# A second, smaller set of staging places, filled by GpSimd's queue, in the opening of a decoder layer

## The chip, the cores and the metric

The kernel runs on one core of a Trainium2 chip. The metric is the device time of one execution in microseconds (us), here of that core. The times of a kernel are given as the median over several runs.

## The reference

One decoder layer over 2048 tokens of width 1024, in float32. Cut to what matters:

```python
mem_n = rmsnorm(mem, mem_norm_g)                       # 256 memory tokens
h = rmsnorm(x, mix_norm_g)
q, k, v, g, u = split(h @ w_in)                        # 4 x 512 and 512 columns
y_ret  = silu(g) * head_rmsnorm(retention(q, k, v))    # 4 heads, chunks of 128
y_pool = (mean over 2/4/8/16 tokens - u) @ pool_w * pool_scale
x = x + concat(y_ret, y_pool) @ w_out
k, v = split(mem_n @ xa_wkv)                           # attention into the memory
s = (rmsnorm(x) @ xa_wq) @ k.T / 16;  p = softmax(s)   # per head
x = x + (p @ v) @ xa_wo
x = x + conv_glu_ffn(rmsnorm(x))
return rmsnorm(x, final_norm_g)
```

## The kernel before

**Products.** Each float32 operand is kept as a pair, a rounded high part and the rest, and each product is three TensorE passes: high by high (L276), high by low (L277), low by high (L278). A pair is made by a *split*: ScalarE copies the high part (L264, or L267 where a factor per row comes in), VectorE subtracts it from the source to get the low part (L248, or L256 with a factor). A split of a 128x1024 tile thus needs its source in SBUF, a place for the pair, and the two engines one after the other.

**Stages.** The first 118 us or so are the *folds*, products that depend on the memory tokens and the weights alone. `folded_weights` is a generator that runs through them in 29 steps, numbered n = 0 to 28 by the loop around it:

- K0 to K7, the key products, and V0 to V7, the value products, 24 matmuls of 128x256 each: the memory against a tile of `wkv` (L347). Two neighbouring products share a PSUM bank, which is scaled and split into a pair of its own afterwards. The banks rotate: M0's first takes the bank that K0 and K1 had.
- M0 to M3, the score products, 48 matmuls of 128x256: two rows of `wqT` per head against the keys.
- O0 to O3, the output products, 24 matmuls of 128x512 for each row of `wo` against the values.
- W0 to W3, short products of `wout_p` with the pooling weights.

They run in the order K0 to K7, V0, V1, M0, V2, M1, V3, M2, V4, M3, O0, V5, O1, V6, O2, V7, W0, W1, O3, W2, W3. Then come the two halves of 1024 tokens, each with its projections, retention, mixer, attention and feed-forward part, until the end at about 2391 us.

Between the steps of the folds the first half's x is prepared: `load_x_wide` loads tile k (128x1024, 512 KB), splits it with the norm's factors, squares it in place on ScalarE (L658), and adds it to `total` on VectorE, from which the norm is made. Tile k = 0 is itself the start of `total`. The tiles are called at the steps in `x_at`. `value_weights` loads the weights of the first products behind the folds, 512 KB a call, 128 rows at a time in each half of a place; it is called at n = 24 and 25, and twice at n = 27.

**Places.** All these loads, the rows of the folds (`load_tile`, `row_pair`), the x tiles and the value weights, go into one set of nine places of 128x1024 float32, `raws`: three in the tile R, the two tiles S (S_80, S_81 below), four in the first arena of Z (Z_75 below). `take` gives the place that was freed first by the order in which the program is written; whoever takes it waits until its last reader has gone. x0 keeps its place until the norm (n = 21), the memory tokens keep two until their norm.

**Queues.** All of these loads are issued by SyncE (SP), one after the other; an issue that waits for its place holds up those behind it. GpSimd's queue has nothing until the sums of weights in DRAM (`weight_sums`, L1055 and L1058, with small copies, L1075) that belong to the stage behind the folds.

**Order.** The Tile framework orders the instructions of each engine by a simulated timeline of its own; `keep_in_program_order` holds some instructions in the order in which they are written: an x tile's load, its split, its square and its sum among them. So a change in one load can put products of TensorE into another order.

Of the kernel before, what the change touches and what calls it, by code (L numbers as in the profile page):

```python
# [16 lines left out]
P = 128  # L17
# [4 lines left out]
T = 1024  # L22
# [120 lines left out]
def trunk(ctx, tc, xT, memT, pos, w_qkgu, w_v, wkv, wqT, wo, wout_r, wout_p, poolT, w_up, w_dn, vecs, consts, outT):  # L143
    nc = tc.nc
    pe, act, dve, pool, sp = nc.tensor, nc.scalar, nc.vector, nc.gpsimd, nc.sync
# [14 lines left out]
    def new_e(at, dtype):  # L160
        return Arena(cp.tile([P, 2 * T], dtype, tag=f"E{at}", name=nm("E")), 0, 2, T)

    def new_s(dtype, at):
        return cp.tile([P, T], dtype, tag=f"S{at}", name=nm("S"))

    B = Joined(Arena(G, 16 * T, 12, T), new_e(0, F32R), new_e(1, F32R))

    def new_z(at, dtype):
        return Arena(cp.tile([P, 4 * T + (0 if at else 4 * EDGE)], dtype, tag=f"Z{at}", name=nm("Z")), 0, 4, T)

    Z = Joined(new_z(0, F32), new_z(1, F32))
    TT = Arena(cp.tile([P, TEMPS * TW], F32, tag="T", name="T"), 0, TEMPS, TW)
    R = cp.tile([P, 3 * T], F32, tag="R", name="R")
    Q = cp.tile([P, 3 * T], F32R, tag="Q", name="Q")
    S = [new_s(F32, j) for j in range(2)]
    raws = Places([(R, j * T) for j in range(3)] + [(r, 0) for r in S], T)
# [70 lines left out]
    def tt(eng, out, a, b, op):  # L247
        return eng.tensor_tensor(out=out, in0=a, in1=b, op=op)  # L248
# [12 lines left out]
    def split(src, hi, lo, g=None, kept=False):  # L261

        if g is None:
            one = act.activation(hi, src, AF.Copy)  # L264
            two = tt(dve, lo, src, hi.bitcast(F32), ALU.subtract)
        else:
            one = act.activation(hi, src, AF.Identity, scale=g)  # L267
            two = stt(lo, src, g, hi.bitcast(F32), ALU.mult, ALU.subtract)
        if kept:
            tc.keep_in_program_order(one)  # L270
        if kept == "both":
            tc.keep_in_program_order(two)
# [7 lines left out]
    def new_raw():  # L280
        r = raws.take()
        r.free()
        return r.f
# [367 lines left out]

    def load_x_wide(k, total):

        r = total if k == 0 else raws.take()
        f = r.f
        tc.keep_in_program_order(sp.dma_start(f, xT[k * P : (k + 1) * P, :T]))
        split(f, X[:, 2 * k], X[:, 2 * k + 1], mixg[:, k : k + 1], kept="both")
        tc.keep_in_program_order(act.activation(f, f, AF.Square))  # L658
        if k:
            tc.keep_in_program_order(tt(dve, total.f, total.f, f, ALU.add))  # L660
            r.free()
# [66 lines left out]
            sp.dma_start(rope_d[i], r.f[:, :SUB])  # L728
            r.free()

    def value_weights(kp, where=None):
        raw = new_raw()
        sp.dma_start(raw.rearrange("p (k n) -> p k n", k=2), w_v[2 * kp : 2 * kp + 2].rearrange("k p n -> p k n"))
        u = (B if where is None else B.arenas[where]).take(2)
        for i in range(2):
            r = raw[:, i * SUB : (i + 1) * SUB]
            split(r, u.r[:, i * T : i * T + SUB], u.r[:, i * T + SUB : (i + 1) * T])
        return u
# [1273 lines left out]
    def rows_norm(s_acc):  # L2012
        rn = smp.tile([P, 8], F32, tag="rn", name=nm("rn"), bufs=3)
        dve.tensor_copy(rn, stats([r.f[:, : r.f.shape[1] // SUB * SUB] for r in s_acc]))
        for r in s_acc:
            r.free()
        return rn
# [67 lines left out]
        after(2, step)  # L2085

    under[0], spacing[0] = weight_sums(), 2
    raws = Places([(R, j * T) for j in range(3)] + [(r, 0) for r in S] + [(Z.arenas[0].t, j * T) for j in range(4)], T)
    results = Places([(Z.arenas[1].t, j * T) for j in range(4)], T)
    wv, total, x_at = [], raws.take(), (5, 10, 12, 13, 14, 16, 17, 18)  # L2090
    for n, _ in enumerate(folded_weights()):
        if n in x_at:
            load_x_wide(x_at.index(n), total)
        if n == 21:
            total.back = None
            rn = rows_norm([total])
        if n in (24, 25):
            wv.append(value_weights(len(wv), 0))
        if n == 27:
            wv += [value_weights(kp, kp - 1) for kp in (2, 3)]  # L2100
    rb = [TT.take() for _ in range(NS)]
    normed = (rn, rb)
    behind[0] = spread_steps(rn, [r.f[:, :SUB] for r in rb])
# [1 line left out]
    for b in range(NB):  # L2105

        if b == 0:
            raws = Places([(R, j * T) for j in range(3)] + [(r, 0) for r in S], T)
# [74 lines left out]
        for n in TURNS[first:]:  # L2183
            if n == TURNS[first]:
                raw = ahead
            else:
                raw = new_raw()
# [3 lines left out]
            if n in (5, 2, 3):  # L2191
                j = (5, 2, 3).index(n)
# [39 lines left out]
        wv, acc, place = [], [], Joined(new_e(0, F32), new_e(1, F32))  # L2232

        def opening():
            for kp in range(KT // 2):
                if kp > 1:
                    B.arenas[kp - 1] = new_e(kp - 2, F32R)
                with tc.issue_after(fetched[0].ins):
                    wv.append(value_weights(kp, (0, 0, 1, 2)[kp]))
                yield  # L2240
                yield
# [96 lines left out]
    raws = Places([(raws.one[i].t, raws.one[i].base + j * SUB) for i in raws.freed for j in range(2)], SUB)  # L2338
    E = [new_e(j, F32R).t for j in range(2)]
    Z = [new_z(j, F32).t for j in range(2)]  # L2340
# [114 lines left out]
```

## Time and profile before

| what | value |
|---|---|
| runs | 2396.65, 2393.47, 2395.16 us; median 2395.16 |
| profiled execution | 2392.77 us, its span 2391.0 us |
| mean granted TensorE clock | 0.998 of full speed |
| busy share of the span | TensorE 99%, its weight load 83%, VectorE 75%, ScalarE 58%, GpSimd 14% |
| DMA | 527.78 MB, mean 221 GB/s |

The span is what the profile's rows cover; the execution's time has 1.8 us more around it. Rows of the order of time hold the start in us, the duration, the engine, the line, the operation, the output and the inputs by the program's names without their numbers, and in brackets the idle time of the engine just before, with what ended it. "PE" is TensorE, "DVE" VectorE, "ACT" ScalarE, "POOL" GpSimd, "SPq" the instructions with which SP issues transfers. R, S and Z in such a row can be any of the places above.

### The profile page before, as it was taken

The numbers are of one execution on the slowest core, as the hardware profiler recorded it, in microseconds if no ns is written. First come the engines' busy times: TensorE is split into PE (matmuls) and PEld (weight loads), VectorE is DVE, ScalarE is ACT, GpSimd is POOL, SyncE is SP. The second block draws the span as 40 slices with busy tenths as digits, with TensorE's granted clock in tenths as the row PEclk, the third lists the DMA queues.
The fourth block names the chain that finished last, engine by engine and source line by source line (L and its number), as shares of the span: only waits on it lengthen the run. The fifth ranks groups of instructions, "written<-read, shape, count | busy, mean of one in ns | idle before, by whom it ended". The sixth has DMA issues, their size and how long they took to land.

```text
span 2391.0 us, 33436 instructions
## 1 busy us (share of the span) xinstructions
PE 2370.1 (99%) x11136; PEld 1981.2 (83%) x11136; DVE 1795.9 (75%) x2977; ACT 1387.2 (58%) x2507; POOL 337.1 (14%) x524
## 2 busy tenths in 40 slices
PE   9999999999999999999999999999999999999998
PEld 8788888888888888888888888888888888888886
DVE  7777776885667677776788776977677698867876
ACT  6854554664445455536555555855555577666663
POOL 0055554454041000000001010110000000000000
PEclk9999999999999999999999999999999999999999
DMA  8999999999595234477467564765455479758952
GB/s 305 332 280 295 275 259 288 298 296 313 179 249 134 80 107 166 155 270 236 168 235 258 176 195 132 251 202 176 152 177 187 132 259 318 235 181 287 342 174 74
DMA packets 269453, 527.78 MB, mean 221 GB/s; under 512 B 30048, under 2 KB 50912, under 8 KB 269280
## 3 DMA queue, kind: packets, MB, share of 16 engines
q1 hardware_dynamic: 212176, 402.83, 50.7%
q0 software_dynamic: 40960, 94.40, 16.6%
q10 hardware_dynamic: 16144, 28.43, 3.2%
q8 instruction: 87, 1.43, 0.2%
q14 instruction: 86, 0.70, 0.1%
HBM read 423.30 MB, written 196.61 MB: 259 GB/s over the span
## 4 chain that ended last, share of the span: by engine, by line
PE 92%; DMA 4%; DVE 2%; ACT 1%; issue 1%; SPq 0%; ACTq 0%; DVEq 0%
PE mm L276 29%; PE mm L278 29%; PE mm L277 29%; PE aux L276 1%; PE aux L278 1%; PE aux L277 1%; DMA S<-w_v 1%; PE aux L804 1%; PE aux L778 1%; PE aux L789 1%; PE aux L951 1%; PE aux L806 1%; PE aux L357 0%; DMA R<-wout_r 0%; DMA R<-Md 0%
## 5 line engine op out<-in xcount | busy, mean ns | idle before, releaser
L276 PE MATMUL mm<-G,Q 128*128 128x512 f32 (+1 forms) x1445 | 559.3, 388 | 6.0 <-ACT Q L264 2.3
L277 PE MATMUL mm<-G,Q 128*128 128x512 f32 (+1 forms) x1445 | 559.3, 387 | 0.3 <-DVE G L256 0.2
L278 PE MATMUL mm<-G,Q 128*128 128x512 f32 (+1 forms) x1445 | 555.8, 387 | 0.0
L277 PE MATMUL mm<-G,E 128*128 128x512 f32 (+1 forms) x1072 | 409.3, 382 | 0.0
L276 PE MATMUL mm<-G,E 128*128 128x512 f32 (+1 forms) x1072 | 408.3, 382 | 0.9 <-ACT E L264 0.5
L278 PE MATMUL mm<-G,E 128*128 128x512 f32 (+1 forms) x1072 | 407.6, 382 | 1.0 <-DVE E L248 1.0
L276 PEld LDWEIGHTS mm<-G,Q 128*128 128x128 f32 x1445 | 272.0, 188 | 62.3 <-ACT Q L264 2.7
L277 PEld LDWEIGHTS mm<-G,Q 128*128 128x128 f32 x1445 | 272.1, 188 | 54.6 <-DVE G L256 0.7
L278 PEld LDWEIGHTS mm<-G,Q 128*128 128x128 f32 x1445 | 271.7, 188 | 54.2 <-DVE Q L248 0.2
L248 DVE TENSOR_TENSOR Z<-Z,mm 128x512 f32<-128x512 f32 (+1 forms) x290 | 193.1, 670 | 92.8 <-PE mm L278 91.2
L256 DVE SCALAR_TENSOR_TENSOR Z<-Z,vecs,Z 128x1024 f32<-128x1024 f32 x176 | 224.5, 1279 | 50.6 <-ACT Z L1223 47.2
L278 PEld LDWEIGHTS mm<-G,E 128*128 128x128 f32 x1072 | 201.3, 188 | 40.6 <-DVE E L248 1.4
L276 PEld LDWEIGHTS mm<-G,E 128*128 128x128 f32 x1072 | 201.4, 188 | 40.3 <-DVE Z L248 0.7
L277 PEld LDWEIGHTS mm<-G,E 128*128 128x128 f32 x1072 | 201.5, 188 | 39.1
L248 DVE TENSOR_TENSOR Q<-R,Q 128x512 fp32r<-128x512 f32 (+2 forms) x206 | 141.0, 685 | 88.0 <-ACT Q L1160 46.9
L248 DVE TENSOR_TENSOR T<-T 128x512 f32<-128x512 f32 (+4 forms) x196 | 133.7, 688 | 28.3 <-ACT T L424 13.6
L1160 ACT ACTIVATE Q<-R 128x512 fp32r<-128x512 f32 (+1 forms) x123 | 75.8, 617 | 131.7 <-PE mm L277 126.1
L1160 ACT ACTIVATE E<-R 128x512 fp32r<-128x512 f32 (+1 forms) x163 | 100.3, 615 | 71.5 <-PE mm L277 56.8
L1223 ACT ACTIVATE Z<-Z,vecs 128x1024 f32<-128x1024 f32 x88 | 109.1, 1241 | 33.8 <-DVE Z L248 32.8
L1107 ACT ACTIVATE G<-T 128x512 fp32r<-128x512 f32 x180 | 108.1, 623 | 34.5 <-DMA T<-Gd 24.9
L1160 ACT ACTIVATE Q<-S 128x512 fp32r<-128x512 f32 (+1 forms) x81 | 49.9, 616 | 97.6 <-PE mm L277 95.2
L248 DVE TENSOR_TENSOR Q<-S,Q 128x512 fp32r<-128x512 f32 (+1 forms) x112 | 75.8, 677 | 37.9 <-ACT Q L1160 26.5
(425 smaller groups left out, 4415.8 us busy)
## 6 DMA issues: line engine op xcount, KB each, us to landing
T<-Gd SPq DMA_DIRECT2D x168, 256.0 KB, 4.5
Ud<-w_up POOLq DMA_DIRECT2D x132, 256.0 KB, 9.9
Gd<-Z SPq DMA_DIRECT2D x110, 256.0 KB, 2.6
R<-Ud SPq DMA_DIRECT2D x104, 256.0 KB, 2.7
R<-w_up SPq DMA_DIRECT2D x82, 256.0 KB, 2.9
S<-Ud SPq DMA_DIRECT2D x72, 256.0 KB, 2.8
Gd<-T SPq DMA_DIRECT2D x56, 256.0 KB, 3.4
T<-Xd SPq DMA_DIRECT2D x53, 256.0 KB, 4.2
```

The source lines that it names most:

```text
L248: return eng.tensor_tensor(out=out, in0=a, in1=b, op=op)
L256: return dve.scalar_tensor_tensor(out=out, in0=a, scalar=s, in1=b, op0=op0, op1=op1)
L276: pe.matmul(ps, lh, rh, start=start, stop=False, skip_group_check=more)
L277: pe.matmul(ps, lh, rl, start=False, stop=False, skip_group_check=more)
L278: latest[0] = pe.matmul(ps, ll, rh, start=False, stop=stop, skip_group_check=more)
L778: pe.matmul(col(sc, c), self.ch(k, c), self.ch(q, c), start=True, stop=True)
L789: pe.matmul(col(kv, c), col(self.kn.f, c), self.ch(v, c, h * T), start=True, stop=True)
L804: pe.matmul(col(y, c), col(self.pr.f, c), self.ch(v, c, h * T), start=True, stop=self.cur[c] is None)
L806: pe.matmul(col(y, c), self.ch(q, c), self.cur[c], start=False, stop=True)
L1107: one = act.activation(hi, x, AF.Copy, scale=-1.0 if i == 2 else 1.0)
L1160: act.activation(p2[:, 0, :w], self.raw[i].f[:, :w], AF.Copy)
L1223: act.activation(self.c[g].f, a[:, 2:], AF.Identity, bias=cb[:, f : f + 1], scale=cw[2][:, f : f + 1])
```

## The change

The x tiles and the four loads of value weights get a set of places of their own, `side_raws`, two of the four in Z's arena; `raws` keeps seven. These loads are issued by GpSimd instead of SP. x0 still goes into `total`, which is taken from `raws`.

```diff
     def load_x_wide(k, total):
 
-        r = total if k == 0 else raws.take()
+        r = total if k == 0 else side_raws.take()
         f = r.f
-        tc.keep_in_program_order(sp.dma_start(f, xT[k * P : (k + 1) * P, :T]))
+        tc.keep_in_program_order(pool.dma_start(f, xT[k * P : (k + 1) * P, :T]))
...
-    def value_weights(kp, where=None):
-        raw = new_raw()
-        sp.dma_start(raw.rearrange("p (k n) -> p k n", k=2), w_v[2 * kp : 2 * kp + 2].rearrange("k p n -> p k n"))
-        u = (B if where is None else B.arenas[where]).take(2)
+    def value_weights(kp, where, side=False):
+        if side:
+            r = side_raws.take()
+            r.free()
+            raw = r.f
+        else:
+            raw = new_raw()
+        (pool if side else sp).dma_start(raw.rearrange("p (k n) -> p k n", k=2), w_v[2 * kp : 2 * kp + 2].rearrange("k p n -> p k n"))
+        u = B.arenas[where].take(2)
...
-    raws = Places([(R, j * T) for j in range(3)] + [(r, 0) for r in S] + [(Z.arenas[0].t, j * T) for j in range(4)], T)
+    raws = Places([(R, j * T) for j in range(3)] + [(r, 0) for r in S] + [(Z.arenas[0].t, j * T) for j in range(2)], T)
+    side_raws = Places([(Z.arenas[0].t, j * T) for j in (2, 3)], T)
...
-            wv.append(value_weights(len(wv), 0))
+            wv.append(value_weights(len(wv), 0, True))
         if n == 27:
-            wv += [value_weights(kp, kp - 1) for kp in (2, 3)]
+            wv += [value_weights(kp, kp - 1, True) for kp in (2, 3)]
```

GpSimd's instructions before, from the program's opening on. `halo` is a small buffer of the convolution, `Ad` the sums of weights in DRAM:

```order
L2451 UNCONDITIONAL_BRANCH
L1075 COPY halo<-halo 128x2
L1058 DMA Ad<-w_qkgu 128x512 x4
L1075 COPY halo<-halo 128x2
L1055 DMA Ad<-w_qkgu 128x512 x2
```

The same stretch of GpSimd's instructions in the changed kernel, whose lines are numbered five higher from L738 on:

```order
L2457 UNCONDITIONAL_BRANCH
L656 DMA R<-xT 128x1024
L656 DMA Z_75<-xT 128x1024 x7
L738 DMA Z_75<-w_v 128x2x512 x4
L1080 COPY halo<-halo 128x2
L1063 DMA Ad<-w_qkgu 128x512 x4
```

The eight x tiles and the four loads of value weights now stand ahead of all sums of weights. x0, x1 and x2 have nothing to wait for, and x3 waits until VectorE has added x1 to `total`.

SP's issues before, in the middle of the folds, where the rows of the score products M1 to M3 (`wqT`) and the first of the output products (`wo`) are asked for:

```order
L474 DMA S_81<-wqT 128x1024
L656 DMA R<-xT 128x1024
L474 DMA Z_75<-wo 128x1024
L474 DMA Z_75<-wqT 128x1024
L656 DMA Z_75<-xT 128x1024
L474 DMA S_81<-wo 128x1024
L656 DMA Z_75<-xT 128x1024
L474 DMA Z_75<-wqT 128x1024
```

And in the changed kernel, the same rows:

```order
L474 DMA S_80<-wqT 128x1024
L474 DMA R<-wqT 128x1024
L474 DMA S_81<-wqT 128x1024
L474 DMA R<-wqT 128x1024
L347 DMA Z_75<-wkv 128x1024
L474 DMA R<-wqT 128x1024
L474 DMA Z_75<-wo 128x1024
```

The x tiles have left SP's list, each row takes the place that another row has left, and the two tiles of x in front of the last row of `wqT` are gone.

TensorE's matmuls before, in the middle of K7, the last key product. `mm14` is the bank of K6 and K7, `G_72` holds the memory's pairs, `E0_73` and `E1_74` the pairs of key weights:

```order
L277 MATMUL mm14_340<-G_72,E0_73 128x256
L278 MATMUL mm14_340<-G_72,E0_73 128x256
L276 MATMUL mm14_340<-G_72,E1_74 128x256
L277 MATMUL mm14_340<-G_72,E1_74 128x256
L278 MATMUL mm14_340<-G_72,E1_74 128x256
```

The same rows in the changed kernel, where `mm18` is the bank of V0:

```order
L277 MATMUL mm14_340<-G_72,E0_73 128x256
L278 MATMUL mm14_340<-G_72,E0_73 128x256
L276 MATMUL mm18_408<-G_72 128x256
L277 MATMUL mm18_408<-G_72 128x256
L278 MATMUL mm18_408<-G_72 128x256
```

K6 ends on E0 in both. In the changed kernel all 24 matmuls of V0 and two of V1 stand ahead of the last key product K7, which before ran ahead of V0.

ScalarE's copies before, behind K7 and up to the results of M0 (`mm19` onward). L387 sets up the keys' scale; `mm7`, `mm8`, `mm13` and `mm14` are the banks of the keys, S4_80 and S5_81 two rows:

```order
L387 ACTIVATE T_77<-aux17_396 128x256
L264 ACTIVATE G_72<-S4_80 128x1024
L264 ACTIVATE G_72<-mm7_146 128x2x256
L264 ACTIVATE G_72<-mm8_203 128x2x256
L264 ACTIVATE G_72<-mm13_281 128x2x256
L264 ACTIVATE G_72<-mm14_340 128x2x256
L264 ACTIVATE G_72<-S5_81 128x1024
L264 ACTIVATE G_72<-mm18_408 128x2x256
L568 ACTIVATE Z3_76<-mm19_477 128x512
```

The same copies in the changed kernel:

```order
L387 ACTIVATE T_77<-aux17_396 128x256
L264 ACTIVATE G_72<-R_78 128x1024
L264 ACTIVATE G_72<-mm18_408 128x2x256
L264 ACTIVATE G_72<-mm7_146 128x2x256
L264 ACTIVATE G_72<-mm8_203 128x2x256
L264 ACTIVATE G_72<-mm13_281 128x2x256
L264 ACTIVATE G_72<-mm14_340 128x2x256
L568 ACTIVATE Z3_76<-mm19_477 128x512
```

The values' bank `mm18` (V0 and V1) is now split ahead of the four banks of the keys instead of behind them, and the second row's split has moved further back.

## What was predicted

> **What bounds the kernel now.** I read the head of the page first, then the busy time by stage, then TensorE in order of time with what ended each idle stretch.
>
> ```profile
> span 2391.0 us, 33436 instructions
> PE 2370.1 (99%) x11136; PEld 1981.2 (83%) x11136; DVE 1795.9 (75%) x2977; ACT 1387.2 (58%) x2507; POOL 337.1 (14%) x524
> ```
>
> ```profile
> 3.00:10.00 7.00, 6.54 (x32) 5.38 (x32) 4.98 (x13) 4.99 (x11) 0.00 (x0) 1.00 1.03 357
> 10.00:30.00 20.00, 19.77 (x162) 19.40 (x162) 16.28 (x30) 13.93 (x15) 0.00 (x0) 1.00 1.03 391
> 70.00:75.00 5.00, 4.28 (x23) 4.28 (x24) 4.29 (x5) 5.00 (x7) 0.00 (x0) 0.66 0.92 333
> 118.00:2391.00 2273.00, 2262.12 (x10405) 1881.44 (x10405) 1710.26 (x2854) 1297.97 (x2387) 336.90 (x520) 1.00 0.70 216
> ```
>
> The columns of the second fence are the stretch, its length, busy time of TensorE, weight load, VectorE, ScalarE and GpSimd, granted clock, DMA share and GB/s. TensorE bounds the program, and after 118 us it hardly waits (2262 of 2273 us busy), with the same matmuls in both kernels. The change acts on the folds, the first 118 us. There TensorE stands at seven places:
>
> ```profile
> 38.04 0.28 PE L278 MATMUL mm<-G 128*128 128x256 f32 x1
> 39.69 0.36 PE L276 MATMUL mm<-G,Q 128*128 128x256 f32 x1 [1.37 <-DVE G L248]
> 59.93 0.39 PE L276 MATMUL mm<-G 128*128 128x256 f32 x1 [1.30 <-DVE G L248]
> 68.07 0.28 PE L277 MATMUL mm<-G 128*128 128x256 f32 x1
> 68.19 0.28 PE L278 MATMUL mm<-G 128*128 128x256 f32 x1
> 70.72 0.39 PE L276 MATMUL mm<-G,Q 128*128 128x256 f32 x1 [2.25 <-ACT Q L264]
> 91.47 0.39 PE L276 MATMUL mm<-G,E 128*128 128x256 f32 x1 [0.54 <-ACT E L264]
> 92.73 0.38 PE L278 MATMUL mm<-G,E 128*128 128x256 f32 x1 [0.76 <-DVE E L248]
> 108.30 0.50 PE L276 MATMUL mm<-G 128*128 128x512 f32 x1 [0.69 <-ACT Z L615]
> 117.96 0.49 PE L276 MATMUL mm<-G,Q 128*128 128x512 f32 x1 [1.27 <-ACT Z L587]
> ```
>
> The brackets hold the idle time and who ended it: 8.2 us in all. Two neighbouring starts (68.07, 68.19) give the pace of a 256-column matmul, 0.12 us. The longest stop costs more than its 2.25: in the stretch from 70 to 75 us the clock is 0.66 and 23 matmuls take 4.28 us instead of 23 x 0.12 = 2.8, so a stop of that length costs 1.5 us again at a low clock, while those of 1.3 us, by the pace after them, cost nothing more. All that the change can win is thus about 8.2 + 1.5 = 9.7 us, 0.4%.
>
> **The change, part by part.**
>
> *The first three x tiles start at once.* In the old order SP issued them one by one:
>
> ```profile
> 3.73 0.47 SPq L347 DMA_DIRECT2D S<-wkv  x1
> 7.83 0.33 SPq L656 DMA_DIRECT2D R<-xT  x1
> 26.78 0.33 SPq L656 DMA_DIRECT2D Z<-xT  x1
> 9.78 1.15 ACT L264 ACTIVATE E<-S 128x512 fp32r<-128x512 f32 x2 [0.24 <-DMA S<-wkv]
> 123.87 2.25 POOL L1058 DMA_DIRECT2D Ad<-w_qkgu  x4
> ```
>
> GpSimd's queue was empty until 123 us; now x0, x1 and x2 stand first in it with no wait, and four issues in a row cost 2.25 us, 0.56 each, so by about 2.5 us all three are out. They are 3 x 512 KB = 1.57 MB. The second tile of key weights (issued at 3.73) is what ScalarE waits for at 9.78, and K1, the second key product, starts on it at about 10.5. The DMA engines are full from 3 us to 30 (share 1.03), so what x takes, the folds lose: 1.57 MB at 391 GB/s is 4.0 us. Part of it falls into the idle moment before 3 us; I take +3.7. The bounds are 0, if GpSimd's packets get through only behind SP's, and 4.0 + 1.5 = +5.5, if the longer wait before K1 also drops the clock. Six key products of 24 x 0.12 = 2.9 us follow K1, with their rows asked for well ahead, so I take it that no later wait shrinks in return, and the delay travels on.
>
> *The order around M0, the first score product.* It waits for a chain that starts at the end of K7, the last key product (31.83 us in the old trace), because it takes over the PSUM bank of the first two key products and these are scaled and split late:
>
> ```profile
> 31.83 0.28 PE L276 MATMUL mm<-G 128*128 128x256 f32 x1
> 34.91 0.39 ACT L387 ACTIVATE T<-aux 128x256 f32<-128x256 f32 x1 [0.98 <-PE aux L382]
> 31.91 1.06 ACT L264 ACTIVATE E<-Z 128x1024 fp32r<-128x1024 f32 x1 [1.82 <-PE mm L277]
> 33.01 1.23 DVE L248 TENSOR_TENSOR E<-Z,E 128x1024 fp32r<-128x1024 f32 x1 [1.32 <-ACT E L264]
> 35.33 2.49 DVE L248 TENSOR_TENSOR mm<-mm,T 128x512 f32<-128x512 f32 x4
> 37.73 1.21 DVE L248 TENSOR_TENSOR G<-S,G 128x1024 fp32r<-128x1024 f32 x1
> 38.86 1.28 DVE L248 TENSOR_TENSOR G<-mm,G 128x512 fp32r<-128x512 f32 x2
> ```
>
> The first row is V0's first matmul, right behind K7's last. Old: 39.69 - 31.83 = 7.9 us, covered by V0 and V1 (50 matmuls, 6.0 us) and standing for the rest, 1.5 us at the pace. New: V0 and two matmuls of V1 stand ahead of K7's end, 26 x 0.12 = 3.1 us of cover lost. The chain after K7 by the new order: ScalarE splits a row (1.06), VectorE follows (1.23, until 2.4), four scalings (2.49, until 4.9), a row (1.2, until 6.1), the split of the values' bank, which now comes first (0.6), and then that of the keys (0.6): 7.4 us. The row at 4.9 is ready by then, since it needs V1's end at 2.9. So M0 starts 7.5 us after K7 with 2.9 us of cover: the stop is 4.6 us instead of 1.5. On the path that is 3.1 of cover less 0.4 of shorter chain, +2.7. A stop of 2.25 us dropped the clock for 1.5 us; this one is longer, so another +1.5: +4.2. Bounds: 0, if K7 ends no later against V0's cover than the scheduler wrote it, and 3.1 + 1.5 = +4.6.
>
> *Rows no longer wait for x's places.* The stops at 70.72 and 91.47 both go back to SP:
>
> ```profile
> 57.35 0.33 SPq L474 DMA_DIRECT2D S<-wo  x1
> 62.23 0.33 SPq L656 DMA_DIRECT2D Z<-xT  x1
> 63.37 0.33 SPq L474 DMA_DIRECT2D Z<-wqT  x1
> 82.30 0.33 SPq L347 DMA_DIRECT2D R<-wkv  x1
> 62.12 1.22 DVE L248 TENSOR_TENSOR R<-R,Z 128x1024 f32<-128x1024 f32 x1
> 81.05 1.23 DVE L248 TENSOR_TENSOR R<-R 128x1024 f32<-128x1024 f32 x1 [0.30 <-ACT R L658]
> 69.62 1.06 ACT L264 ACTIVATE Q<-Z 128x1024 fp32r<-128x1024 f32 x1 [2.17 <-DMA Z<-wqT]
> 90.36 1.06 ACT L264 ACTIVATE E<-R 128x1024 fp32r<-128x1024 f32 x1 [0.82 <-DMA R<-wkv]
> ```
>
> SP issues nothing from 57.7 to 62.2, then an x tile, then at 63.37 M3's row, in the place that an x tile held until its sum ended at 62.12 + 1.22 = 63.34; the row lands at 69.6 and TensorE stood for it. The same at 82.30: its place was free when an x sum ended at 82.28. In the new order every place of a row is freed by a row's split, six rows back, so both rows are asked for earlier than ScalarE can use them. I take both stops away: from 68.19 to 70.72 are 2.53 - 0.12 = 2.4, with 1.5 of low clock 3.9; and 0.54 + 0.76 = 1.3. Together -5.2. Bounds: 0 and -5.2. What is late next are the x tiles themselves, each asked for only when the tile two back is summed, and the last value weights (below).
>
> The Trainium skill, page "DMA: Bandwidth & Descriptors", section "Issuing engines are not separate DMA queues", speaks against this step: issuing from several engines saves only the issue time, since the 16 engines are the same. By that alone the sum would lose its -5.2 and be +7.9. The rows above show a queue standing for a place and not for bandwidth, which that rule leaves out; it gets the chance of the fourth rival.
>
> *The other stops.* 59.93 hangs on the split of a values' bank behind an x tile's split; the new order has the same neighbours there: 0 (bounds -1.3 and +1). 108.30 and 117.96 (2.0 together) wait for ScalarE's copies at the end; x7 and the value weights are now split between the same copies: 0, from -2.0 to the second rival's price. Issue time saved on SP (12 x 0.33 to 0.42) and spent on GpSimd (12 x 0.56 = 7 us) is on nobody's path: GpSimd did nothing there, and its first sums waited until 123 us for ScalarE, which comes there no sooner.
>
> **Sum.** +3.7 + 4.2 - 5.2 = +2.7 us. The profiled execution took 2392.77 us (span 2391.0 and 1.8 around it), so 2395.5 by its own time. It lies 2.4 under the median of the runs, 2395.16, against which I forecast 2397.9. A measurement of this kernel can tell about 0.2%, 4.8 us: this is no change that can be told.
>
> **The rivals.**
>
> 1. *Faster: x's first tiles cost nothing.* If GpSimd's packets wait behind SP's, the start costs 0 to 0.5, the clock stays up in the shorter stop at M0 (+2.7), and with every transfer earlier the stops at 59.93, 108.30 and 117.96 (3.3) go too: 0.5 + 2.7 - 5.2 - 3.3 = -5.3, 2389.9. For it: GpSimd's first issue. Against: x's rows are asked for at the same moment as the folds' and the engines are full. Chance 0.15.
>
> 2. *Slower: the second value weights come late.* They wait in GpSimd's queue until the last x tile is summed on VectorE, at the end of the output folds; by the new order TensorE then has about 7.5 us until it needs them (half of the last output fold, 16 sums, W2, W3, 6 matmuls of the values), of which 0.6 go to the issue and 0.6 to the split. The point is a landing of 6.3 us. Rows of GpSimd's queue:
>
> ```profile
> Ud<-w_up POOLq DMA_DIRECT2D x132, 256.0 KB, 9.9
> Ad<-w_qkgu POOLq DMA_DIRECT2D x11, 256.0 KB, 6.9
> ```
>
> At 9.9 us TensorE stands 3.6 and, past 2.25, 1.5 at the low clock: +5.1, in all +7.8, 2403.0. Chance 0.20. By the same skill page, section "Anatomy of one DMA — SWDGE (gpsimd) path", 512 KB take an estimated 2.0 + 1.2 = 3.2 us, and this rival would not exist; the rows here, beside other traffic and for half the bytes, are two to three times that, and count.
>
> 3. *The start at half clock.* If TensorE stands so long before K1 that the clock falls, the start is +5.2: +4.2, 2399.4, on the border to slower. Chance 0.13. Against it: stops of 1.3 us cost no clock.
>
> 4. *The change doesn't do what it says:* the rows of M3 and V7 are still late, because six places are fewer than the eight shared ones, and the stops stay: +7.9, 2403.1. Chance 0.10. Against: the new places free earlier.
>
> **How the numbers follow.** The forecast gets 0.42, its own range 2394 to 2400. Slower by over 0.2% (above 2400.0): rivals 2 and 4, half of 3: 0.37. Faster (below 2390.4): rival 1, 0.15. The rest 0.48. For eight in ten the range reaches down to 2388, past rival 1, and up to 2406, past rivals 2 and 4 with a start at its upper bound.
>
> **What would show it.** Right, in the changed trace: three x issues on GpSimd before 3 us; ScalarE's split of the second key tile at about 13.5 instead of 9.78; a stop of 4 to 5 us before M0 with a clock near 0.5 behind it; no stop for rows of wqT or wkv later. Wrong: that split still near 10 us; M0 waiting under 2 us; a stop behind the value weights' transfer, or TensorE standing for an x tile's evaluation on ScalarE between 75 and 118 us; or any stop after the first values, where I expect none.

## The result and the profile after

| | median, us | runs, us |
|---|---|---|
| before | 2395.90 | 2393.47 to 2396.98 (4) |
| changed | 2409.62 | 2408.19 to 2412.57 (4) |

The ratio is 1.006, with a 95% interval of 1.0043 to 1.0078: 13.7 us slower, beyond the range that was forecast (2388 to 2406). The profiled execution of the changed kernel is its slowest (2412.57 us), that of the kernel before one of its fastest (2392.77), so the two profiles lie 19.8 us apart, some 6 of them between executions of one kernel.

By stage, in the columns of the prediction's second fence, in the changed kernel, whose span is 2410.8 us:

```profile
3.00:10.00 7.00, 4.22 (x17) 3.40 (x16) 1.91 (x6) 1.69 (x4) 0.07 (x1) 1.00 1.04 346
40.00:60.00 20.00, 14.45 (x99) 14.03 (x98) 11.24 (x14) 11.04 (x16) 0.00 (x0) 0.83 0.38 112
118.00:130.00 12.00, 10.34 (x45) 7.88 (x44) 7.89 (x21) 5.66 (x10) 0.73 (x1) 1.00 1.01 367
130.00:200.00 70.00, 64.44 (x269) 51.62 (x268) 55.41 (x98) 34.61 (x73) 39.72 (x57) 0.95 0.93 251
595.00:615.00 20.00, 17.50 (x70) 13.65 (x69) 7.20 (x12) 5.72 (x10) 2.70 (x4) 0.91 0.83 204
```

These are the stretches in which TensorE loses. Its stops of over 1 us, in order of time, with what ended each, and one short stop at 122.54 that is needed below:

```profile
10.41 0.58 PE L276 MATMUL mm<-G,Q 128*128 128x256 f32 x1 [2.60 <-ACT G L267]
48.19 0.55 PE L276 MATMUL mm<-G,Q 128*128 128x256 f32 x1 [5.55 <-DVE G L248]
122.54 0.50 PE L276 MATMUL mm<-G 128*128 128x512 f32 x1 [0.31 <-ACT G L264]
128.27 0.50 PE L276 MATMUL mm<-G 128*128 128x512 f32 x1 [1.35 <-ACT Z L615]
174.59 0.79 PE L278 MATMUL mm<-G,Q 128*128 128x512 f32 x1 [4.05 <-DVE Q L248]
608.11 0.50 PE L276 MATMUL mm<-Z,Q 128*128 128x512 f32 x1 [1.75 <-ACT Q L264]
```

Around the one at 174.59 lie two shorter ones, 0.66 us at 169.18 and 0.85 at 182.83. At the start, GpSimd's issues of x, ScalarE's split of the memory tokens' second piece and that of the second key tile, and the step of TensorE from K0 to K1, the first product that reads that tile (`E`):

```profile
1.29 0.71 POOL L656 DMA_DIRECT2D R<-xT  x1 [0.84 <-POOLq L2453]
1.99 1.08 POOL L656 DMA_DIRECT2D Z<-xT  x2
9.85 0.91 ACT L267 ACTIVATE G<-R,vecs 128x256 fp32r<-128x256 f32 x2 [3.63 <-DMA R<-memT]
14.02 1.15 ACT L264 ACTIVATE E<-S 128x512 fp32r<-128x512 f32 x2 [0.31 <-DMA S<-wkv]
15.38 0.41 PE L278 MATMUL mm<-G,Q 128*128 128x256 f32 x1
15.59 0.41 PE L276 MATMUL mm<-G,E 128*128 128x256 f32 x1
```

The second key tile's split came at 9.78 before. The stops of the kernel before at 59.93, 70.72, 91.47 and 92.73 us are gone. Those at 10 and 48 us are the start and M0. The one at 128.27 is of the kind of the old one at 108.30, ended by the same copy of ScalarE; those from 169 us on have none like them in that profile of the kernel before.

Both kernels run the same 11136 matmuls, so the cleanest measure is how much later the n-th matmul of TensorE's list starts than in the first profile of the kernel before, counting from 0. The table is worked out that way, from one profiled execution each. The chosen n lie behind K1, M0, M3, the folds, the first weights' products, at the end of the first half and in the second. The experiments are told below; two more profiles of the kernel before (e9, e14) show how far executions alone differ.

| n (start before, us) | 100 (18.2) | 300 (44.1) | 540 (79.7) | 731 (118.0) | 1200 (222.0) | 2950 (579.6) | 5000 (1002.1) |
|---|---|---|---|---|---|---|---|
| changed kernel | +4.7 | +11.2 | +5.6 | +2.5 | +14.8 | +14.4 | +18.6 |
| e9, e14: before again | -0.2, +0.4 | -0.2, +0.4 | -0.5, -0.6 | -0.2, +0.5 | +0.1, +0.3 | +4.0, +0.1 | +4.3, +3.0 |
| e1: value weights back | +4.8 | +10.0 | +4.7 | +4.8 | +4.6 | +5.1 | +4.7 |
| e2: same places, by SP | +5.2 | +9.9 | +4.4 | +3.2 | +9.1 | +8.9 | +10.3 |
| e3: by GpSimd, shared places | +4.3 | +10.7 | +5.1 | +4.2 | +3.9 | +3.4 | +9.6 |
| e4: hold that did not hold | +4.6 | +9.3 | +3.8 | +2.1 | +14.1 | +13.5 | +14.6 |
| e5: e1, x held | +1.3 | +8.1 | +2.5 | +2.0 | +1.7 | +2.0 | +9.9 |
| e6: e1, K7 first | +4.9 | +4.4 | -1.1 | -2.7 | -3.0 | -2.8 | +3.0 |
| e7, e15: both | +0.8, +1.2 | +0.7, +1.2 | -4.8, -4.3 | -6.6, -6.2 | -6.9, -6.4 | -7.4, -6.9 | +1.6, +7.5 |
| e8: e1, x by SP | +1.0 | +6.4 | +0.8 | -1.0 | -1.2 | -1.7 | +5.0 |
| e10: queue alone | +0.9 | +0.9 | +2.1 | +0.7 | +0.5 | +1.1 | +2.1 |
| e11: three places | +7.1 | +15.9 | +10.4 | +6.5 | +6.4 | +6.0 | +8.0 |
| e12: e7, fewer additions | +1.7 | +1.6 | -4.0 | -5.2 | -5.4 | -5.9 | -6.2 |
| e13: e7, sums early | +1.8 | +4.2 | -1.4 | +11.9 | +21.6 | +24.9 | +31.7 |

At the end of the folds the changed kernel is 2.5 us late, and the forecast for that point was 2.7. Then it loses 12 us between 118 and 222 us, most of it from 169 us on, and 4 near 600.

**What happens behind the folds.** The value weights pass through the two places behind the x tiles. GpSimd's issues, the splits and the first work of the next stage:

```profile
104.07 0.73 POOL L738 DMA_DIRECT2D Z<-w_v  x1 [6.15 <-DVE R L248]
113.11 1.22 DVE L248 TENSOR_TENSOR R<-R,Z 128x1024 f32<-128x1024 f32 x1
114.63 0.73 POOL L738 DMA_DIRECT2D Z<-w_v  x1 [9.82 <-DVE R L248]
123.21 0.69 DVE L248 TENSOR_TENSOR G<-Z,G 128x512 fp32r<-128x512 f32 x1
124.40 0.73 POOL L738 DMA_DIRECT2D Z<-w_v  x1 [7.86 <-DVE yh L395]
131.51 1.29 DVE L248 TENSOR_TENSOR E<-Z,E 128x512 fp32r<-128x512 f32 x2 [1.46 <-ACT E L264]
132.73 0.69 DVE L248 TENSOR_TENSOR R<-R 128x512 f32<-128x512 f32 x1
158.09 0.33 SPq L1841 DMA_DIRECT2D S<-w_qkgu  x1
164.63 0.69 DVE L248 TENSOR_TENSOR R<-S,R 128x512 f32<-128x512 f32 x1 [3.05 <-DMA R<-w_qkgu]
173.85 0.68 DVE L248 TENSOR_TENSOR Q<-S,Q 128x512 fp32r<-128x512 f32 x1
```

It reads as one chain. The second value weights are asked for when x7's sum ends (113.11 + 1.22 = 114.33, issue at 114.63). The fourth go into the place of the second, whose split ends at 123.21 + 0.69 = 123.9; the issue comes at 124.40, right behind a small cast of the norm that follows that split, and they are split at 131.51. Behind that split in VectorE's list stands the first difference of x's quarters (132.73), the work of the next stage. The places of those quarters come free late, so SP asks for the next weights (`w_qkgu`) at 158.09; VectorE stands for them until 164.63, has its list to work off, and splits them at 173.85. TensorE waits for that at 174.59. The same points before:

```profile
108.88 0.38 SPq L733 DMA_DIRECT2D S<-w_v  x1
118.17 1.28 DVE L248 TENSOR_TENSOR E<-S,E 128x512 fp32r<-128x512 f32 x2
119.37 0.68 DVE L248 TENSOR_TENSOR R<-R 128x512 f32<-128x512 f32 x1
142.34 0.33 SPq L1836 DMA_DIRECT2D S<-w_qkgu  x1
```

The last value weights were asked for 15.5 us earlier there, the next stage's weights 15.8 us earlier.

### The profile page after: what moved, and what is told of

Its sections match the earlier page's. It is cut to its first block, busy times and chain, and to the rows that moved or that the text cites. A ratio compares the mean times of both kernels' runs of the same rounds, so it can differ in the third digit from the quotient of the medians.

```text
span 2410.8 us, 33429 instructions
## 1 busy us (share of the span) xinstructions
PE 2379.7 (99%) x11136; PEld 1986.9 (82%) x11136; DVE 1797.8 (75%) x2977; ACT 1386.9 (58%) x2507; POOL 346.9 (14%) x536
## 4 chain that ended last, share of the span: by engine, by line
PE 92%; DMA 3%; DVE 2%; ACT 1%; issue 0%; SPq 0%; DVEq 0%; ACTq 0%
PE mm L276 29%; PE mm L278 28%; PE mm L277 28%; PE aux L276 1%; PE aux L278 1%; PE aux L277 1%; PE aux L809 1%; PE aux L783 1%; PE aux L794 1%; PE aux L956 1%; DMA R<-w_qkgu 1%; PE aux L811 1%; DMA WPd<-Z 1%; DMA S<-w_v 1%; DVE Z L248 0%; PE aux L357 0%
## 5 line engine op out<-in xcount | busy, mean ns | idle before, releaser
L276 PEld LDWEIGHTS mm<-G,E 128*128 128x128 f32 x1072 | 202.2, 189 | 39.6 <-DVE Z L248 0.7
L248 DVE TENSOR_TENSOR Q<-S,Q 128x512 fp32r<-128x512 f32 (+2 forms) x116 | 80.8, 697 | 38.1 <-ACT Q L1165 26.3
```

The lines of the kernel that those rows point to most:

```text
L276: pe.matmul(ps, lh, rh, start=start, stop=False, skip_group_check=more)
```

## The experiments

All are edits of the changed kernel; e5, e6 and e8 start from e1, their base, and e12 and e13 from e7. Ratios are to the kernel before on the same chip.

**e1, e2, e3: queue or places for the value weights.** e1 calls `value_weights` without `side`, so that they go to SP and the shared places. e2 and e3 split this in two:

```diff
 # e2: own places, SP
-        (pool if side else sp).dma_start(raw.rearrange(...
+        sp.dma_start(raw.rearrange(...
 # e3: GpSimd, shared places
-            r = side_raws.take()
-            r.free()
-            raw = r.f
+            raw = new_raw()
```

> The four value weights go back to SP's queue and to the shared (seven) places; x's tiles stay on their two places and on GpSimd's queue. Theory P (places): in the changed kernel x6, x7 and the four value weights pass through two places one behind the other, so the last value weights are split at 131.5 us; ScalarE and VectorE take their instructions in order, so the first difference of x's quarters stands at 132.7 instead of 119.4, the weights of the next stage are asked for at 158 instead of 142, and TensorE stops at 169 to 206 us for 10 us. By P those stops go here: the first difference of the quarters at 122 us or before, about +2.5 us against the kernel before at the end of the folds and nothing behind them, 2396 to 2400 us. Theory N (norm): it is x's own tiles, whose last sum ends at 114 us, that hold the stage up; then nothing changes here: 2407 to 2411 us, the first difference still at about 132.

> The value weights keep the two places of their own and are issued by SP instead of GpSimd. Theory P (two places): no better, 2406 to 2412 us, last value weights split at about 131 us. Rival Q (queue): they are late because they are issued by GpSimd, whose queue holds x's tiles ahead of them and whose transfers take about 7 us to land; then this gives 2396 to 2400 us.

> The value weights are still issued by GpSimd, into the seven shared places instead of the two. Theory P: the late stage goes, 2396 to 2401 us. Rival Q (queue): no better than the changed kernel, 2407 to 2411 us.

Measured: e1 2400.01 us, 1.0014 (1.0004 to 1.0024); e2 2404.81, 1.0035 (1.0024 to 1.0046); e3 2400.69, 1.0015 (1.0006 to 1.0025). All stops between 128 and 206 us are gone in e1 and e3. With the two places they stay by either queue, but not alike: between matmuls 731 and 1200 the changed kernel loses 12.2 us, e4, its second look, 12.0, and e2, with SP as the issuer, 5.9. So the two places are needed for the loss: with shared places GpSimd as the issuer does no harm (e3 against e1), while with two places about half of the loss goes with it (by the medians, on one chip, e2 is 3.6 us faster than e4). e2 thus lies between what theory P (2406 to 2412) and rival Q (2396 to 2400) gave for it. GpSimd's four loads of value weights take 6.8 us to land at the median, as against 6.7 by SP before.

Two points of the chain stay open. The first difference of the quarters still stands at 130.87 in e1, not at 122 as expected, only 1.9 us ahead of the changed kernel; but SP asks for `w_qkgu` at 152.26, 5.8 us ahead of it. Between the two points VectorE stands idle for 3.8 us in the changed kernel (2.35 of them at 137.16, for ScalarE) while in e1 it has no such idle time. A request 10 us later than before costs TensorE nothing in e1 and e3 (152.90), and one 16 us later comes with 12 us lost. e2 asks at 152.82, like e3, and its stops hang on something else, VectorE's wait for the rotary tables (`rope_d`), which are stored in DRAM and read back. I have not followed that wait back to the two places:

```profile
186.82 0.71 DVE L248 TENSOR_TENSOR T<-T 128x525 f32<-128x525 f32 x1 [4.37 <-DMA rope_d<-T]
189.40 0.50 PE L276 MATMUL mm<-G,Q 128*128 128x512 f32 x1 [2.83 <-DVE T L248]
```

**e4: a hold that did not hold.** The loads of x0 to x2 were written inside `tc.issue_after(...)` of matmuls of K1, K5 and V0.

> The changed kernel, with GpSimd's loads of x0, x1 and x2 held until the ends of K1, K5 and V0 on TensorE. Theory B (bytes at the start): the 1.57 MB of x beside the first key rows are what delays K1; held, the second key tile is split at 9.8 to 10.3 us instead of 14.0 and the whole run gains 4 to 5 us against the changed kernel, 2404 to 2406 us. Rival M (moved): the rows of K2 to M0 now give way to the same bytes a little later, the delay comes back as stops before M0, and the gain is under 1.5 us, 2408 to 2410 us.

```profile
1.28 0.71 POOL L657 DMA_DIRECT2D R<-xT  x1 [0.83 <-POOLq L2456]
```

The issues came as early as in the changed kernel, x1 and x2 from 1.98 us on: the construct made GpSimd wait for nothing. e4 tells nothing on its question. It is a second look at the changed kernel: 2408.37 us, 1.0045 (1.0028 to 1.0062), with the same ladder, and only 1.1 us lost near 600.

**e5, e6, e7: the start and M0.** e5 puts a real dependency ahead of x0, x1 and x2; e6 writes V0 behind K7; e7 has both.

```diff
 # e5: gate[k] is the low part of K1's, K4's and K7's pair
+        if k < 3:
+            tc.keep_in_program_order(pool.tensor_copy(halo[:, 41 + k], gate[k][:, :2].bitcast(F32)))
 # e6: in project(n)
+            with tc.issue_after(latest[0].ins) if n == KT else nullcontext():
```

> Value weights on SP and the shared places as in e1, and GpSimd's loads of x0, x1 and x2 truly held: ahead of each stands a small copy on GpSimd of a piece of the split of K1's, K4's and K7's weights. In e4 the hold had only changed the order of issue, and x was asked for at 1.3 us as in the changed kernel. Theory B (x's bytes delay the first rows): the second key tile is split at 9.8 to 10.3 us instead of 14, and matmul 100 of TensorE starts within 1 us of the kernel before, not 4.7 behind it. By the new order only 9 matmuls are left between K7 and M0, so M0's stop grows to 6.5 to 7.5 us. In sum 2396 to 2399 us. Rival D (depth): the start is late because SP has two places fewer and asks for the rows of K4 and K5 later; then the split stays near 14 us, and the sum is 2401 to 2403 us.

> e1 with V0's matmuls written to be issued behind K7's last, so that 48 matmuls of the values stand between K7 and M0 as in the kernel before, instead of 22. Theory C (cover): the chain behind K7 takes about 8.2 us, the 48 matmuls cover 5.8 of it, so M0's stop is 2 to 2.8 us instead of 5.3 and the low clock behind it is gone: 4 us faster than e1, 2395 to 2397 us. Rival R (late row): M0 waits because the row of wqT is asked for at 34.4 us only, lands at 40.4 and heads ScalarE's queue; then the order on TensorE changes little, the stop stays at 4 us or more, 2399 to 2401 us.

> e5 and e6 together. If B and C hold, the start and M0's stop are as in the kernel before, and the stops for rows at 70 and 91 us (4 and 1.7 us) stay away: 2390 to 2394 us, faster than the kernel before by 0.1 to 0.25%. If D or R holds: 2395 to 2400 us.

The split of the second key tile in e5, then M0's first matmul in e6, against 14.02 and 48.19 [5.55] in the changed kernel:

```profile
10.14 0.63 ACT L264 ACTIVATE E<-S 128x512 fp32r<-128x512 f32 x1 [0.30 <-DMA S<-wkv]
```

```profile
44.14 0.35 PE L276 MATMUL mm<-G,Q 128*128 128x256 f32 x1 [0.52 <-DVE G L248]
```

e5: theory B holds. With x held the split is at 10.14 and matmul 100 is 1.3 us late, not 4.8, so x's bytes make the start late and not the smaller number of places. M0's stop grew to 5.20 + 1.08 us, as its 9 covering matmuls said. The time, 2401.88 us and 1.0016 (1.0007 to 1.0025), is no better than e1 and misses the 2396 to 2399 expected, since 8 us go near 600. e6: theory C holds, and rival R does not: with 48 covering matmuls M0 waits 0.52 us, less than the 2 us expected at the least, and the low clock is gone; 2396.43 us, 0.9995 (0.9985 to 1.0004). e7 is 6.6 us ahead at the end of the folds, and measures 2394.40, 0.9988 (0.9979 to 0.9998).

**e8, e10: is it the queue or the places that frees the rows?** e8 is the base with x by SP, in its own two places. e10 is the changed kernel with `side_raws = raws`, nine shared places, all x and value weights by GpSimd.

> e1 with x's tiles issued by SP again, into the two places of their own: places without the queue. If the rows' stops went because of the places, there is no stop for a row between 60 and 95 us here either; if the separate queue did it, the x issues that wait on SP hold up rows again and the stops come back, 2 us or more in all. The start is as in the kernel before (second key tile split by 10.3 us). All 48 matmuls of V0 and V1 stand ahead of K7's end here, none behind it, so by theory C M0's stop is 7.5 to 8.5 us, and the run 2398 to 2401 us; by rival R the stop is about 5 us as in e1 and the run 2393 to 2396 us.

> The changed kernel with one set of nine places again: x's tiles and the value weights are still issued by GpSimd, but take turns with the rows. Theory P (two places cause the late value weights): no stop of TensorE from 128 to 210 us. x0 alone can start at once, the others wait for places, so the start costs 1 to 2 us instead of 4.7; V0's first matmuls stand behind K7, so M0's stop is 1 to 3 us; the stops for rows at 70 and 91 us go if it was SP's queue that held the rows. 2394 to 2399 us. Rival Q (queue): GpSimd's queue makes the value weights late whatever their places, 2404 us or more.

M0 in e8, and in e10 the row of `wqT` that TensorE stood for at 70.72 before:

```profile
42.32 0.58 PE L276 MATMUL mm<-G,Q 128*128 128x256 f32 x1 [3.29 <-ACT G L264]
44.08 0.58 PE L277 MATMUL mm<-G,Q 128*128 128x256 f32 x1 [1.17 <-DVE G L248]
```

```profile
73.22 0.58 PE L276 MATMUL mm<-G,Q 128*128 128x256 f32 x1 [2.78 <-ACT Q L264]
```

With places of its own and SP as issuer (e8) no row is waited for between 60 and 95 us. With GpSimd's queue and shared places (e10) that stop stays, 2.78 us. So the rows were held by x tiles that sat in their places, and not by x issues ahead of them on SP: SP's queue, which e10's expectation had left as a possibility, was not the cause, and the queue alone does nothing, 2397.08 us, 0.9998 (0.9988 to 1.0008). That agrees with the Trainium skill, page "DMA: Bandwidth & Descriptors", section "Issuing engines are not separate DMA queues". e10 also has no stop from 128 to 210 us, as theory P says. e8 measured 2397.44, 0.9999 (0.9988 to 1.0010). Its M0 stopped for 4.5 us, nearer to the 5 of rival R than to the 7.5 to 8.5 of C; between the two e6 decides, not e8. With all of V0 and V1 ahead of K7, ScalarE had split a row and the values' bank before K7 ended, so the chain behind K7 was shorter. The chain has no fixed length; it holds whatever stands ahead of it in ScalarE's and VectorE's lists.

**e11: three places.** `side_raws` gets (1, 2, 3) of Z's arena, `raws` six places.

> The changed kernel with three places of their own for x and the value weights, and six for the rows. Theory P: the chain of the last value weights through the places gets one turn shorter, so the last are split about 7 us earlier (near 124 us) and TensorE's stops from 169 to 206 us shrink from 10 us to under 3; x3 starts at once too, so the start costs 5 to 7 us. V0's first 28 matmuls stand ahead of K7 and 20 behind it: M0's stop is about 5 us as before. In sum 2399 to 2405 us. Rival Q: the value weights stay late, 2408 us or more.

2402.13 us, 1.0019 (1.0008 to 1.0030). The last value weights are split at 127.70 to 129 us, and no stop is left between 118 and 250 us, 3 to 5 us later than expected and early enough. The start costs 7.1 us with four x tiles at once, and 5 us more go before K7, with six places for the rows: TensorE stops 3.18 us at 36.54 for a late tile of `wkv`.

**e9 and e12 to e15: what is lost at 600 us.** Near 600 us the second half's rows of VWd and value weights are loaded by SP, while the last of GpSimd's sums of weights before that half still run. e12 leaves the additions out of the second half of the sums of `w_up` (the copies stay). e13 starts the sums in the folds, by `next(under[0], None)` from n = 18 on.

> The kernel before, unchanged, for a second profile of it. In e3 and e5 to e8 TensorE lost 6 to 9 us between 600 and 625 us, where the second half's rows of VWd and value weights land while GpSimd's sums of weights still run; the one profile of the kernel before shows no stop there. Theory F (fluke): that profile, 2392.8 us, was one of its fastest executions, and a more usual one shows a stop of 1 to 4 us there too and 2395 to 2400 us. Rival G (given back): the kernel before has no such stop, and the gains of e5 to e8 in the folds are what is lost there; then this profile shows none again, 2392 to 2394 us.

> e7 with part of GpSimd's work left out: for the second half of the sums of w_up the copies in DRAM stay and the additions are left out, so the feed-forward products use weights that are not the sums. Theory S (sums): e7 is 7 us ahead of the kernel before until 590 us and loses 9.4 us from 595 to 615, because the sums of weights, whose pace the DMA engines set, then still run beside the second half's loads of VWd and value weights (VWd's row took 9.6 us to land, 3.7 in the kernel before). With the sums done earlier, TensorE stops for under 1.5 us in all between 580 and 625 us, and is still 5 us or more ahead of the kernel before at 1000 us. Rival O (order): the loads are late because of their place in SP's list, behind two x loads that wait 12 us for their buffers; then the stops there stay at 4 us or more.

> e7 with GpSimd's sums of weights begun in the folds, from n = 18 on, one turn for two steps, about five turns ahead of the folds' end. By theory S their end comes some 5 to 10 us earlier against TensorE's work, half or more of the 9.4 us at 600 us stays won, and the run takes 2388 to 2392 us, unless the sums' bytes delay the last rows of the folds (DMA share 0.83 to 1.06 there). By rival O nothing is won at 600 us, 2394 to 2397 us.

> The kernel before, unchanged, on the same chip as e15. e5 to e8 and e12 ran on another chip than e9, so that e9 cannot say what the kernel before loses at 600 us beside them. Theory H (head start): it loses under 2 us there on any chip. Rival K (chip): where e15 loses 5 us or more, this kernel loses 3 us or more too.

> e7 again, beside a profile of the kernel before on the same chip. Theory H (the head start won in the folds brings TensorE to the second half's loads while the sums still run): 4 us or more lost between 580 and 625 us, on this chip as on that of e7, and 0.05 to 0.2% faster than the kernel before. Rival K (the loss belongs to the chip): if this chip is that of e1 to e4 and e9, under 2 us lost and 0.25 to 0.3% faster; if it is that of e7, the kernel before loses there too.

The last sum issued by GpSimd ahead of the second half, the row of VWd, and what waited for it: before, then e7; then the row alone in e12. TensorE behind it in e7 and e15 (last two fences).

```profile
590.53 0.81 POOL L1055 DMA_DIRECT2D Dd<-Dd  x1 [4.90 <-DMA Dd<-Dd]
596.30 0.33 SPq L347 DMA_DIRECT2D R<-VWd  x1
599.95 0.63 ACT L264 ACTIVATE Q<-R 128x512 fp32r<-128x512 f32 x1 [2.36 <-DMA R<-VWd]
```

```profile
588.20 0.33 SPq L347 DMA_DIRECT2D R<-VWd  x1
595.50 0.81 POOL L1065 DMA_DIRECT2D Dd<-Dd  x1 [5.87 <-DMA Dd<-Dd]
597.78 0.63 ACT L264 ACTIVATE Q<-R 128x512 fp32r<-128x512 f32 x1 [8.30 <-DMA R<-VWd]
```

```profile
583.21 0.33 SPq L347 DMA_DIRECT2D R<-VWd  x1
...
586.60 0.63 ACT L264 ACTIVATE Q<-R 128x512 fp32r<-128x512 f32 x1 [1.78 <-DMA R<-VWd]
```

```profile
598.46 0.70 PE L276 MATMUL mm<-Z,Q 128*128 128x512 f32 x1 [2.99 <-ACT Q L264]
607.64 0.50 PE L276 MATMUL mm<-Z,Q 128*128 128x512 f32 x1 [1.82 <-ACT Q L264]
```

```profile
601.30 0.50 PE L276 MATMUL mm<-Z,Q 128*128 128x512 f32 x1 [1.43 <-ACT Q L264]
613.29 0.79 PE L276 MATMUL mm<-Z,Q 128*128 128x512 f32 x1 [5.95 <-ACT Q L264]
```

Before, SP asked for the row 5.8 us behind the last sum; in e7, 7.3 us ahead of it. From issue to ScalarE's start the row took 3.7 us, 9.6 us and 3.4 us. In e12, with the sums done earlier, nothing is lost at 600 us and the 5.9 us won stay: 2387.28 us, 0.9950 (0.9935 to 0.9965), part of which is the additions left out. Theory S holds for e7: the sums, not the order of SP's list. e13 misses altogether: 2424.82 us, 1.0104 (1.0082 to 1.0127). ScalarE's stores of the folds' results, beside the sums' bytes, took up to 19 us to land (97.24 to 116.20; in e7 at most 9.9), x7's sum came at 121.98, and TensorE stood 7.30 us for the norm; at 600 us it still lost 7. It says nothing for or against S.

e9 (2398.27 us) shows no stop at 600 us and is 4 us late from another place, between 297 and 483 us, so F failed as I worded it, and G by its time. e14 (2395.85) loses 2.9 us at 600. e15, on e14's chip, loses 14.4 us there in its profile, which is the slowest of its 11 executions (2400.3; the others 2390.3 to 2398.0), and is faster by its median: 2393.94 us, 0.9978 (0.9967 to 0.9988). So the loss at 600 us differs from execution to execution and is there in the kernel before too. It is largest in the two profiles that arrive 7 us early (9.0 us in e7, 14.4 in e15), but e5, which arrives 2 us late, loses 7.9, and e1, 5 us late, nothing. How much of it in e7's median is head start and how much chance stays open.

e7 is the fastest version with no work left out, and beats both kernels: 0.12% and 0.22% under the kernel before on two chips.

## Why the prediction was wrong

- *Start, +3.7 (0 to +5.5).* Right in its cause and near in size, +4.7 at matmul 100: three x issues stand on GpSimd before 3 us, and e5 shows that it is x's bytes. The wait is another than the one that I named. The split of the second key tile, forecast at 13.5, came at 14.02, but K1 starts at 15.59 right behind K0, with no stop. TensorE had stood inside K0, 2.60 us at 10.41, for the second piece of the memory tokens, and from there to 16.2 us it ran at 0.21 us a matmul (15.38 to 15.59) at best, instead of 0.12. So part of the +4.7 is the slow pace of my third rival.
- *M0, +4.2 (0 to +4.6).* Right mechanism, mis-sized: +6.5, from 4.7 to 11.2 in the ladder. The term took the stop for 4.6 us and 1.5 us of low clock; they were 5.55, and 2.7 by the ladder between the stop's end and matmul 300. K7 ends at 39.6, so M0 starts 8.6 us behind it where I had 7.5, with the 2.9 us of cover that I gave. (The old stop, which I put at 1.5, is 7.9 - 6.0 = 1.9 by the numbers beside it; the +2.7 goes by the 1.9.) Two things in the chain had no term. One is a row that I took for ready, split 0.9 us behind K7's end; the other is VectorE's half of the split of a tile of `wkv`, which stands between that row and the scalings:

```profile
34.36 0.33 SPq L474 DMA_DIRECT2D R<-wqT  x1
...
40.47 1.06 ACT L264 ACTIVATE G<-R 128x1024 fp32r<-128x1024 f32 x1 [5.71 <-DMA R<-wqT]
42.70 1.22 DVE L248 TENSOR_TENSOR E<-Z,E 128x1024 fp32r<-128x1024 f32 x1
```

  The row heads ScalarE's list and was asked for at 34.36 only. Whether the smaller number of places made it late stays open: e8 has the same seven, and splits a row at 36.08, ahead of K7's end.
- *Rows, -5.2 (-5.2 to 0).* Right: no stop for a row of `wqT` or `wkv` is left; the lag falls from 9.6 us at matmul 480 to 3.8 at 620, by 5.8 us. e8 and e10 show that the places did it: I spoke of a standing queue too, and SP stood because places were taken.
- *59.93, 108.30 and 117.96, 0.* Too careful: about -1.5 and -1.3. These make up for M0, and so the sum at the end of the folds, +2.7, was hit (+2.5) by luck, with errors that cancel.
- *Value weights: the failed step.* "x7 and the value weights are now split between the same copies: 0, from -2.0 to the second rival's price." That rival had the right cause, value weights that wait for the last x tile's sum, but I priced it by TensorE's direct wait for their landing alone, 5.1 us at most. The direct wait was small: 0.31 us at 122.54. (The 1.35 at 128.27 is another wait: ScalarE's copy that ended it had waited for the store of earlier results, `WPd`.) What I left out is who stands behind a late split in the lists of ScalarE and VectorE: the whole of the next stage. I wrote that no stop was to come after the first values; 12 us were lost there. e1 and e3 show that the two places are needed for it, and e11 that a third takes it away. I also set its point by the time of the landing, where the count of places decides: x7, the second and the fourth value weights pass through one place, a chain of three loads, each with its landing and its sum or split, from 97 to 133 us.
- *The rest.* The changed profile loses 4 us near 600 us, which the prediction did not consider. e4, nearly the same kernel, loses 1.1 there, so this is not shown to be the change's price.

The range was too narrow for one reason: the cases that I added up all ended with the folds.

## What to carry to other kernels

A pool of places that is split in two shortens one queue's waits and makes the other's turns a chain: count the loads that must pass through the small part one after the other, with a landing and a split for each, before costing the large part's gain. Price a late operand also by what stands behind it in the list of the engine that prepares it, up to the engine that bounds, and not only by the wait for the operand itself. A gain early in a program can be lost again where the program next meets another engine's work: compare the start of the n-th matmul at several points, and not the end alone.

## What the runs showed of the hardware

- A stop's price in clock is not a matter of its length alone. In the kernel before, stops of 1.37 and 1.30 us (39.69, 59.93) left the granted clock at 1.00, and one of 2.25 (70.72) was followed by 0.66 over 5 us. In e1, with two stops of 1.47 and 1.93 us, 3.3 us apart (8.73 and 12.07), it was 0.50 from 10.5 to 17 us, and in e10 it was 0.50 behind a single stop of 0.92 us at 7.81:

```profile
8.40:11.60 3.20, 3.20 (x14) 3.03 (x15) 2.81 (x7) 2.89 (x7) 0.00 (x0) 0.50 1.04 413
```

- The column of the granted clock is to be read beside the pace. From 12 to 15 us, in the changed kernel and then in e1:

```profile
12.00:15.00 3.00, 2.81 (x12) 2.28 (x12) 2.41 (x6) 2.69 (x6) 0.00 (x0) 1.00 1.03 418
```

```profile
12.00:15.00 3.00, 2.92 (x12) 2.69 (x13) 2.50 (x6) 2.37 (x6) 0.00 (x0) 0.50 1.03 419
```

  The column differs by a factor of two, and yet 12 matmuls ran in both, from 13.5 us on 0.21 us apart. The changed kernel's trace has its first record of the clock at 16.27 us, and there the pace goes from 0.21 to 0.12; ahead of that record the 1.00 tells nothing. e1 reached matmul 100 as late as the changed kernel (4.8 against 4.7 us).
- Executions of one kernel on one chip differ by up to 10 us (the kernel before beside e15: 2394.4 to 2404.9), and its three profiles place part of that: 0 to 3 us at 600 us, and once 4 us between 297 and 483 us.
